# More raw weight tiles and input slots, loads of x and weights ahead of the S5 parameters, roots on GpSimd, in a one-core hybrid block

## The chip, the cores and the metric

One core of a Trainium2 chip runs the whole block in one launch. The metric is the device time in microseconds of that launch. Before the change the median of 3 runs is 1591.73 us (1591.47 to 1593.48). The engines are TensorE (PE; its weight loads are listed apart as PEld), VectorE (DVE), ScalarE (ACT), GpSimd (POOL) and SyncE (SP), which here only issues DMAs.

## The reference

Sequence 1024, width 1024, depth 1, one batch. Cut to what is computed:

```
u = rms_norm(x, norm_mix);  proj = u @ w_in
u_ssm, q, k, v, f_logit, gate_logits = split(proj)        # 512, 512, 512, 512, 8, 2048
y_ssm = gelu(s5_ssm(u_ssm, lam, dt, b, c, d))             # 32 groups of 16, 64 complex states each
glu_a, glu_b = split(y_ssm @ w_glu);  out_a = glu_a * sigmoid(glu_b)
out_b = forgetting_attention(q, k, v, f_logit + b_forget) @ w_fox_o     # 8 heads of 64, causal
gate_a, gate_b = split(sigmoid(gate_logits))
h = x + (gate_a * out_a + gate_b * out_b) @ w_mix_out
h = h + cross_attention(rms_norm(h), rms_norm(mem), w_mem_q, w_mem_kv, w_mem_o)   # 256 tokens, 4 heads
f_a, f_b = split(rms_norm(h) @ w_ffn_in);  h = h + (silu(f_a) * f_b) @ w_ffn_out  # hidden 2816
return rms_norm(h)
```

All is float32.

## The kernel before

**Products.** Every float32 operand of a large product is split in two parts in the matmul type: `hi`, a cast on ACT (L178), and `lo`, the rest, a subtraction on DVE or, where asked for, on GpSimd (L179). A product is then three matmuls, hi·hi, hi·lo and lo·hi (`mm3`, L168 to L170). A weight block goes by DMA into a tile `raw` of the weight pool (0.5 MB for 1024 columns) and from there by a split into `whi` and `wlo`. All places that fetch weights share the tag `raw` with 2 buffers (L150, L383, L559, L803, L1537), so that a load waits until the split two loads before it is done.

**Stages.** `stage_in` normalises and transposes mem and x, computes keys and values of the memory and the S5 input projection. `stage_ssm` computes 32 units of the gates beside the S5 recurrence. Then come the eight heads of forgetting attention, with the Glu products as filler for TensorE, and `stage_tail`: mixing, cross-attention, FFN, output.

**The opening, `stage_in`.** Its work is written as a table of steps, `ORDER_IN` (L41), which is run through from left to right. A letter is the kind of step, what follows is its tile or block (m, n are the two mem tiles, 0 to 7 the x tiles; weights are counted in hexadecimal, so Da and Db are 10 and 11):

- G gain, F fetch of a tile (L349), Q its square sum on ACT (L360), R the root of the mean (L362, for x one for a pair of tiles), S scaling (L217), T transposes on TensorE (L223; half 0 into the one `misc` bank of PSUM, half 1 into `pv`), E their evacuation as hi and lo (`uh`, `ul`)
- D fetch of a weight block (L384): 0 to 3 key columns, 4 to 7 value rows of w_mem_kv, 8 to 11 column blocks of w_in for the S5 input; W its split
- K, k and V, v: key and value products of the memory and their evacuation, ending in stores to `kv_d` (L408, L423)
- U and u: the S5 input product of block q for the half h of the sequence (24 matmuls), and its evacuation; "U10" is block 1, half 0
- L0: 13 small DMAs with the S5 parameters lam, log dt, C, B, d (L1132 to L1148). L1: the transposes of lam and C, through the `misc` bank (L1153, L1160), and their copies on DVE (L1155, L1161). P: the rest of the S5 preparation, mostly on DVE

The framework's scheduler takes this order as priority, and moves single instructions where an engine's operands come later; each engine then runs its own list in order. Tiles of x, mem and the two gains share the tag `xt` with 8 buffers (L347).

**Queues.** SyncE issues nearly all loads, in order. Its DMAs go round eight completion lanes: a DMA waits for the landing of the one that used its lane before. An issue that waits for a free buffer or a lane holds up all that follow it.

**Roots.** `rsqrt` (L187) has two ways. With `pool=True` GpSimd raises to the power -0.5 (L197, with the constant tile `mhalf`) and DVE adds one Newton step of three operations; with `pool=False` DVE makes a first guess on the bits (L199) and three Newton steps (L201 to L203). The four roots for the pairs of x tiles in the opening take the second way, all others the first.

Of the kernel before, what the change touches and what calls it, by code (L numbers as in the profile page):

```python
# [9 lines left out]
F32 = mybir.dt.float32  # L10
# [9 lines left out]
P = 128  # L20
D = 1024
# [10 lines left out]
RAW = 1072  # L32
# [6 lines left out]
RSLOT_LATE = (0, 1, 2, 3, 4, 4, 5, 5, 6, 6, 7, 7)  # L39

ORDER_IN = """  # L41
G0 Fm Qm Fn D1 X24 Qn Rm D0 Sm F1 G1 Tm0 Rn Em0 Sn Tn0 F0 Tm1 W0 Q0 Tn1 En0 F2 Q1 W1g En1 Em1 K0 D2 F3 K1 R0
S0 T00 T01 k0 E00 Q2 W2g D3 E01 D4 S1 T10 Q3 W3 k1 D5 K3 K2 W4 E10 W5 D6 R1 k2 T11 k3 S2 F4 Q4 V0 F5 S3g T30
E11 D7 Q5 F7 T20 R2 T21 E21 E20 S4 E30 W6 W7 T40 V1 D8 S5 E40 W8 T31 V2 L0 T41 E31 V3 D9 Db T50 F6 Q6 v T51 W9
E51 U00 Da Q7 L1 E41 u00 R3 S6 Wa T60 E50 S7 T61 T70 Wbg E61 U10 E60 P0 U20 u10 T71 E70 E71 u20 P1 U21 U11 U30
P2 u30 U31 u11 u31 U01 u21 P3 P4 P5 u01
"""

# [57 lines left out]
class Shared:  # L106
# [5 lines left out]
    def tmp(self, name, dt=F32):  # L112
        return self.pool.tile([P, D], dt, tag="tmp", bufs=4, name=name)
# [5 lines left out]
class Block:  # L119
    BANKS = {"mm": 3, "sc": 2, "pv": 2, "misc": 1}  # L120

    def __init__(self, ctx, tc):
        self.tc, self.nc = tc, tc.nc
        nc = self.nc
        self.V, self.A, self.G, self.T, self.S = nc.vector, nc.scalar, nc.gpsimd, nc.tensor, nc.sync
        self.const = ctx.enter_context(tc.tile_pool(name="const", bufs=1))
        self.small = ctx.enter_context(tc.tile_pool(name="small", bufs=3))
        self.wpool = ctx.enter_context(tc.tile_pool(name="wpool", bufs=4))
        self.dram = ctx.enter_context(tc.tile_pool(name="dram", bufs=1, space=DRAM))
        self.psum = ctx.enter_context(tc.tile_pool(name="psum", bufs=2, space=PSUM))  # L130
        self.ident = self.const.tile([P, P], F32, name="ident")
        make_identity(nc, self.ident)
        self.mhalf = self.const.tile([P, 1], F32, name="mhalf")
        nc.vector.memset(self.mhalf, -0.5)
        self.junk = self.const.tile([P, 512], BF16, name="junk")
        self.nbank = 0
# [197 lines left out]
def stage_in(B, xp, s5, x, mem, g_mix, g_kv, w_in, w_mem_kv, uT, u_d, kv_d):  # L334
# [9 lines left out]
    names = {"m": -2, "n": -1, **{str(t): t for t in range(NT)}}  # L344

    def xtile(name="xt"):
        return xp.tile([P, D], F32, tag="xt", bufs=8, name=name)  # L347

    def fetch(t):  # L349
        tiles[t] = xtile()  # L350
# [9 lines left out]
        A.activation(junk, tiles[t], AF.Square, scale=1.0 / 32, accum_out=ss[t // 2][:, t % 2:t % 2 + 1])  # L360
# [15 lines left out]
    def wget(i):  # L376
        if i < 4:
            src = w_mem_kv[:, i * P:(i + 1) * P]
        elif i < 8:
            src = w_mem_kv[2 * (i - 4) * P:2 * (i - 3) * P, 512:1024]  # L380
        else:
            src = w_in[:, C_U + (i - 8) * P:C_U + (i - 7) * P]
        raw[i] = B.wpool.tile([P, RAW], F32, tag="raw", bufs=2, name="raw")[:, :D]  # L383
        S.dma_start(raw[i].rearrange("p (k c) -> p k c", k=D // src.shape[-1]),  # L384
                    src.rearrange("(k p) c -> p k c", p=P))

# [111 lines left out]
def stage_tail(B, big, s2, sh, x, glu, aT, gate_d, kv_d, w_fox_o, w_mix_out, g_mq, w_mem_q, w_mem_o, g_ffn,  # L498
# [10 lines left out]
    tmp = sh.tmp  # L509
# [46 lines left out]
    def wslots(src, pool_lo):  # L556

        nk = src.shape[0] // P
        raw = B.wpool.tile([P, RAW], F32, tag="raw", bufs=2, name="raw")[:, :D]  # L559
# [240 lines left out]
    raws, wts, ev = {}, {}, {}  # L800

    def w_fetch(j):
        raws[j] = B.wpool.tile([P, RAW], F32, tag="raw", bufs=2, name="raw")[:, :D], tmp("rawb")  # L803
# [615 lines left out]
class Fox:  # L1419
# [109 lines left out]
    def project(self, h):  # L1529
# [4 lines left out]

        def load(behind=None):
            src = lambda c: self.w_in[:, c + h * DH:c + (h + 1) * DH].rearrange("(k p) c -> p k c", p=P)
            raw = self.raw[h] = B.wpool.tile([P, RAW], F32, tag="raw", bufs=2, name="raw")[:, :D]  # L1537
# [273 lines left out]
```

## Time and profile before

| | |
|---|---|
| median of 3 runs | 1591.73 us (1591.47 to 1593.48) |
| span of the profiled execution | 1586.7 us, 5.0 us under the median |
| TensorE busy | 1534.0 us, 97% |
| DVE, ACT, GpSimd busy | 1019.5, 655.2, 254.3 us |
| DMA | 240.86 MB, 152 GB/s over the span |

Busy time says for how long an engine had an instruction running. In a timeline row the first number is the start, the second the time in use, and brackets give the idle time ahead of it and what ended it. `SPq` rows are issues of DMAs by SyncE: their second number is the time until the next could follow, waits included. The chain of waits is the work that ended last, followed back from the end. The granted clock is TensorE's, 1.00 at full speed.

### The profile page before, as it was taken

What the parts mean: (1) busy time and instruction counts of PE and PEld (TensorE: products, weight loads), DVE (VectorE), ACT (ScalarE), POOL (GpSimd) and SP (SyncE); (2) the same over time, 40 slices, a digit from 0 to 9 for tenths busy, and PEclk for the clock granted to TensorE, in tenths of its full rate; (3) what the DMA queues carried; (4) which work ended last, traced back from release to release, by engine and by line L of the source; (5) the groups of instructions that cost most, each with busy time, mean ns of one, the idle gap of its engine ahead of it and who ended that gap; (6) DMA issues with size and microseconds to landing.
All of it is one profiled execution on the core that took longest, in us unless ns stands there. A gap on an engine that the chain in (4) does not pass through costs nothing.

```text
span 1586.7 us, 20446 instructions
## 1 busy us (share of the span) xinstructions
PE 1534.0 (97%) x7313; PEld 1261.3 (79%) x7313; DVE 1019.5 (64%) x1850; ACT 655.2 (41%) x1173; POOL 254.3 (16%) x335
## 2 busy tenths in 40 slices
PE   7799999999999899999999999999999999999997
PEld 6578888898777668888888778888888888788885
DVE  6666445344688687675555697766677776565555
ACT  6422434323576553222435564333333333254342
POOL 2027653200212124110002200100000000000001
PEclk8899999999999999999999999999999999999999
DMA  7764445652023736357412186555444554796642
GB/s 266 125 132 80 127 131 110 130 145 30 18 52 48 186 95 208 125 172 259 160 46 75 54 283 239 170 164 163 155 153 160 166 162 156 261 391 223 195 150 106
DMA packets 197940, 240.86 MB, mean 152 GB/s; under 512 B 35448, under 2 KB 126488, under 8 KB 197328
## 3 DMA queue, kind: packets, MB, share of 16 engines
q1 hardware_dynamic: 191216, 223.84, 48.2%
q10 hardware_dynamic: 6624, 15.73, 2.6%
q8 instruction: 57, 0.93, 0.2%
q14 instruction: 43, 0.35, 0.1%
HBM read 165.60 MB, written 75.86 MB: 152 GB/s over the span
## 4 chain that ended last, share of the span: by engine, by line
PE 75%; DVE 8%; DMA 7%; issue 4%; POOL 3%; ACT 2%; SPq 1%; DVEq 0%; POOLq 0%; ACTq 0%
PE mm L868 14%; PE mm L168 7%; PE pv L868 7%; PE mm L170 7%; PE mm L169 7%; PE mm L1005 4%; PE sc L868 3%; PE sc L1005 3%; PE pv L1005 3%; PE sc L168 3%; PE sc L169 3%; PE sc L170 3%; DMA raw<-in_w_in_dram 2%; PE misc L1005 1%; PE pv L168 1%
## 5 line engine op out<-in xcount | busy, mean ns | idle before, releaser
L179 DVE TENSOR_TENSOR wlo<-raw,whi 128x1024 fp32r<-128x1024 f32 (+2 forms) x121 | 132.0, 1094 | 135.1 <-ACT whi L178 133.9
L178 ACT CAST whi<-raw 128x1024 fp32r<-128x1024 f32 (+2 forms) x124 | 116.1, 940 | 220.0 <-DMA raw<-in_w_ffn_in_dram 54.1
L168 PE MATMUL mm<-uh,whi 128*128 128x512 f32 x344 | 138.8, 404 | 2.8 <-ACT whi L178 2.7
L170 PE MATMUL mm<-uh,wlo 128*128 128x512 f32 x344 | 136.5, 397 | 1.7 <-DVE wlo L179 1.7
L169 PE MATMUL mm<-ul,whi 128*128 128x512 f32 x344 | 136.4, 396 | 0.0
L179 DVE TENSOR_TENSOR ol<-or,oh 128x1024 fp32r<-128x1024 f32 x73 | 89.3, 1224 | 71.6 <-ACT oh L178 70.3
L178 ACT CAST oh<-or 128x1024 fp32r<-128x1024 f32 x73 | 76.8, 1052 | 105.3 <-PE mm L1005 33.6
L900 POOL TENSOR_TENSOR g<-a,c 128x512 f32<-128x512 f32 x22 | 35.2, 1600 | 392.8 <-ACT a L899 373.9
L170 PEld LDWEIGHTS mm<-uh,wlo 128*128 128x128 f32 x344 | 65.7, 191 | 16.5 <-DVE wlo L179 3.1
L1630 POOL TENSOR_TENSOR pl<-pf,ph 128x512 fp32r<-128x512 f32 (+1 forms) x32 | 39.7, 1239 | 241.1 <-DVE ph L1629 196.1
L168 PEld LDWEIGHTS mm<-uh,whi 128*128 128x128 f32 x344 | 65.9, 192 | 15.5 <-ACT whi L178 3.2
L169 PEld LDWEIGHTS mm<-ul,whi 128*128 128x128 f32 x344 | 66.0, 192 | 11.3
L197 POOL TENSOR_TENSOR r<-ms,mhalf 128x1 f32<-128x1 f32 x26 | 15.1, 582 | 354.9 <-DVE ms L193 344.5
L1627 ACT ACTIVATE pf<-sc 128x512 f32<-128x512 f32 (+1 forms) x96 | 46.5, 490 | 46.3 <-DVE sc L1623 28.6
L868 PE MATMUL pv<-S3h,we 128*128 128x512 f32 x176 | 58.1, 389 | 0.0
L1633 DVE TENSOR_TENSOR pl<-pf,ph 128x512 fp32r<-128x512 f32 (+2 forms) x64 | 35.1, 550 | 10.2 <-ACT ph L1632 9.5
L1005 PE MATMUL mm<-oh 128*128 128x512 f32 x106 | 41.2, 389 | 0.0
L1005 PE MATMUL mm<-ol,oh 128*128 128x512 f32 x106 | 41.2, 389 | 0.0
L1005 PE MATMUL mm<-oh,ol 128*128 128x512 f32 x106 | 41.2, 389 | 0.0
L168 PE MATMUL mm<-yh,whi 128*128 128x512 f32 x104 | 40.9, 393 | 0.0
L168 PE MATMUL sc<-uh,whi 128*128 128x512 f32 x104 | 40.8, 393 | 0.0
L170 PE MATMUL mm<-yh,wlo 128*128 128x512 f32 x104 | 40.6, 390 | 0.0
(580 smaller groups left out, 4537.5 us busy)
## 6 DMA issues: line engine op xcount, KB each, us to landing
or<-c_d SPq DMA_DIRECT2D x77, 256.0 KB
raw<-in_w_in_dram SPq DMA_DIRECT2D x22, 512.0 KB
wo<-in_w_ffn_out_dram SPq DMA_DIRECT2D x22, 512.0 KB
c_d<-g SPq DMA_DIRECT2D x44, 256.0 KB
t_d<-wo SPq DMA_DIRECT2D x44, 256.0 KB
or<-t_d SPq DMA_DIRECT2D x44, 256.0 KB
raw<-in_w_ffn_in_dram SPq DMA_DIRECT2D x20, 512.0 KB
rawb<-in_w_ffn_in_dram SPq DMA_DIRECT2D x20, 512.0 KB
```

The costliest lines, as they stand in the source:

```text
L168: T.matmul(ps, lh, rh, start=first, stop=False)
L169: T.matmul(ps, lh, rl, start=False, stop=False)
L170: T.matmul(ps, ll, rh, start=False, stop=last)
L178: self.A.copy(hi, src)
L179: (self.G if pool_lo else self.V).tensor_sub(lo, src, f32(hi))
L197: self.G.tensor_tensor(out=r, in0=v, in1=self.mhalf[:, 0:n], op=ALU.pow)
L868: T.matmul(ps, l_[:, k, :], r_, start=first and k == 0 and i == 0, stop=k == 3 and i == 2, skip_group_check=True)
L900: G.tensor_mul(g[:, 512:], a1, c1)
L1005: T.matmul(ps, l_[:, gi], r_[:, 512:], start=n < 3 and p == 0 and k == 0 or n == 7 and p == 0 and k == 0, stop=p == NP - 1 and k == 2, ski ...
L1627: self.exp = A.activation(pf[:, off:], ps[:, off:], AF.Exp)
L1630: G.tensor_sub(pl[:, off:], pf[:, off:], f32(ph[:, off:]))
L1633: V.tensor_sub(pl[:, off:], pf[:, off:], f32(ph[:, off:]))
```

## The change

- The program is built with a reserve of 1024 bytes for GpSimd's DMAs (L1797), in place of the default.
- The tag `raw` has 4 buffers in all its places, `xt` 11 instead of 8.
- `mhalf` is two wide and `root` no longer asks for the DVE way, so that the four roots of x use GpSimd too.
- `ORDER_IN` is another table: fetches of x tiles and of weight blocks come earlier, L0 later, and a few steps behind them in another place.

```diff
 ORDER_IN = """
-G0 Fm Qm Fn D1 X24 Qn Rm D0 Sm F1 G1 Tm0 Rn Em0 Sn Tn0 F0 Tm1 W0 Q0 Tn1 En0 F2 Q1 W1g En1 Em1 K0 D2 F3 K1 R0
-S0 T00 T01 k0 E00 Q2 W2g D3 E01 D4 S1 T10 Q3 W3 k1 D5 K3 K2 W4 E10 W5 D6 R1 k2 T11 k3 S2 F4 Q4 V0 F5 S3g T30
-E11 D7 Q5 F7 T20 R2 T21 E21 E20 S4 E30 W6 W7 T40 V1 D8 S5 E40 W8 T31 V2 L0 T41 E31 V3 D9 Db T50 F6 Q6 v T51 W9
-E51 U00 Da Q7 L1 E41 u00 R3 S6 Wa T60 E50 S7 T61 T70 Wbg E61 U10 E60 P0 U20 u10 T71 E70 E71 u20 P1 U21 U11 U30
+G0 Fm Qm Fn D1 X24 Qn Rm D0 Sm F1 G1 Tm0 Rn Em0 Sn Tn0 F0 D2 Tm1 W0 Q0 Tn1 En0 F2 F3 D3 Q1 W1g En1 Em1 K0 F4 F5 K1 R0
+S0 T00 T01 k0 E00 Q2 W2g D4 F6 F7 E01 S1 T10 Q3 W3 k1 D5 K3 K2 W4 E10 W5 D6 R1 k2 T11 k3 S2 Q4 V0 S3g T30
+E11 D7 Q5 T20 R2 T21 E21 E20 S4 E30 W6 D8 W7 T40 V1 D9 S5 E40 T31 V2 E31 W8 T41 L0 V3 Da T50 Q6 v T51 W9
+E51 U00 Db Q7 E41 R3 S6 u00 L1 Wa T60 E50 S7 T61 T70 Wbg E61 U10 E60 T71 E70 E71 P0 U20 u10 u20 P1 U21 U11 U30
 P2 u30 U31 u11 u31 U01 u21 P3 P4 P5 u01
 """
@@ Block.__init__
-        self.mhalf = self.const.tile([P, 1], F32, name="mhalf")
+        self.mhalf = self.const.tile([P, 2], F32, name="mhalf")
@@ wload; the same in wget, wslots, w_fetch and project's load
-        raw = self.wpool.tile([P, RAW], F32, tag="raw", bufs=2, name="raw")
+        raw = self.wpool.tile([P, RAW], F32, tag="raw", bufs=4, name="raw")
@@ stage_in
-        return xp.tile([P, D], F32, tag="xt", bufs=8, name=name)
+        return xp.tile([P, D], F32, tag="xt", bufs=11, name=name)
...
-        rs[i] = B.rsqrt(ss[-1][:, i % 2:i % 2 + 1] if i < 0 else ss[i], pool=i < 0)
+        rs[i] = B.rsqrt(ss[-1][:, i % 2:i % 2 + 1] if i < 0 else ss[i])
@@ launch
-    nc = _bacc.Bacc("TRN2", target_bir_lowering=False, num_devices=1)
+    nc = _bacc.Bacc("TRN2", target_bir_lowering=False, num_devices=1, dynamic_dma_scratch_size=1024)
```

SyncE's list in the opening, from the w_in block D8 (after: from the second store of K) to D10. Before, the three `raw` rows on in_w_in are D8 (`raw_523`), D9 (`raw_593`) and D11 (`raw_595`), and the last row is D10:

```order
L384 DMA raw_523<-in_w_in_dram 128x8x128
L1141 DMA craw_556<-in_c_re_dram 128x1x64 x3
L1141 DMA craw_561<-in_c_im_dram 128x1x64 x4
L1146 DMA b_re_566<-in_b_re_dram 128x16x16
L1146 DMA b_im_567<-in_b_im_dram 128x16x16
L1148 DMA dbc_570<-in_d_skip_dram 128x512
L384 DMA raw_593<-in_w_in_dram 128x8x128
L384 DMA raw_595<-in_w_in_dram 128x8x128
L351 DMA xt_602<-in_x_dram 128x1024
L423 DMA kv_d_83<-kv_298 128x1024
L423 DMA kv_d_83<-kv_299 128x1024
L384 DMA raw_650<-in_w_in_dram 128x8x128
```

After, D8 and D9 are `raw_486` and `raw_509`, D10 is `raw_579`; D11 (not shown) follows two more stores to kv_d:

```order
L408 DMA kv_d_83<-kv_297 128x1024
L384 DMA raw_486<-in_w_in_dram 128x8x128
L384 DMA raw_509<-in_w_in_dram 128x8x128
L1132 DMA prow_546<-in_lam_re_dram 16x128
L1133 DMA prow_546<-in_lam_im_dram 16x128
L1135 DMA ldr_549<-in_log_dt_dram 16x2
L1141 DMA craw_551<-in_c_re_dram 128x1x64 x4
L1141 DMA craw_556<-in_c_im_dram 128x1x64 x4
L1146 DMA b_re_561<-in_b_re_dram 128x16x16
L1146 DMA b_im_562<-in_b_im_dram 128x16x16
L1148 DMA dbc_565<-in_d_skip_dram 128x512
L384 DMA raw_579<-in_w_in_dram 128x8x128
```

D8 and D9 now stand together ahead of all parameters, and D10 directly behind them; the x tiles have left this part of the list.

DVE's list around the copies of C's transposes (`cT_re`, `cT_im`). Before, the split of W9 (`wlo_618`) comes ahead of them, that of W10 later:

```order
L179 TENSOR_TENSOR wlo_618<-raw_593,whi_617 128x1024
L179 TENSOR_TENSOR ul1_1_98<-misc_597,uh1_1_90 128x2x128
L1155 COPY par_656<-misc_654 128x48
L248 TENSOR_SCALAR edt_xc_750<-par_656 128x16
L1216 TENSOR_TENSOR den_1052<-par_656 128x16
L249 TENSOR_SCALAR edt_k_751<-edt_xc_750 128x16
L250 TENSOR_SCALAR edt_k_751<-edt_k_751 128x16
L1161 COPY cT_re_658<-misc_660 128x256
```

After:

```order
L1252 TENSOR_TENSOR dbc_565<-dbc_565,msk_1064 128x512
L1155 COPY par_653<-misc_651 128x48
L179 TENSOR_TENSOR wlo_666<-raw_579,whi_665 128x1024
L1161 COPY cT_re_655<-misc_657 128x256
L179 TENSOR_TENSOR ul2_1_100<-pv_679,uh2_1_92 128x2x128
L248 TENSOR_SCALAR edt_xc_739<-par_653 128x16
```

The split of W10 (`wlo_666`) now stands between the copy of lam (`par`) and the copies of C.

ACT's list in attention, at the weights of head 7 (`whi_5057` before, `whi_5033` after) and the first Glu weights (`whi_5628`, `whi_5604`). Before:

```order
L178 CAST whi_5057<-raw_4963 128x1024
L1627 ACTIVATE pf_5070<-sc_5064 128x256
L178 CAST whi_5628<-raw_5625 128x1024
L1632 CAST ph_5068<-pf_5070 128x256
L1562 ACTIVATE hb_3246<-mm_4959 64x512
L1627 ACTIVATE pf_5089<-sc_5083 128x128
L1563 CAST hb_3244<-mm_4959 64x512
L1632 CAST ph_5087<-pf_5089 128x128
L1567 ACTIVATE hb_3247<-mm_4959 64x512
```

After:

```order
L178 CAST whi_5033<-raw_4939 128x1024
L1627 ACTIVATE pf_5046<-sc_5040 128x256
L178 CAST whi_5604<-raw_5601 128x1024
L1632 CAST ph_5044<-pf_5046 128x256
L178 CAST whi_5688<-raw_5685 128x1024
L1627 ACTIVATE pf_5065<-sc_5059 128x128
L1562 ACTIVATE hb_3222<-mm_4935 64x512
L1632 CAST ph_5063<-pf_5065 128x128
L1563 CAST hb_3220<-mm_4935 64x512
L178 CAST whi_5773<-raw_5770 128x1024
L1654 COPY num_4858<-pv_4960 65x512
L1567 ACTIVATE hb_3223<-mm_4935 64x512
```

The second and third Glu weights (`whi_5688`, `whi_5773`) stand here now; before, they came some 40 rows later. Their loads on SyncE stand ahead of head 7's forget rows (L1575) for the same reason.

More of the change, by code (lines that the diff above doesn't have):

```diff
@@ L382, in wget @@
             src = w_in[:, C_U + (i - 8) * P:C_U + (i - 7) * P]
-        raw[i] = B.wpool.tile([P, RAW], F32, tag="raw", bufs=2, name="raw")[:, :D]
+        raw[i] = B.wpool.tile([P, RAW], F32, tag="raw", bufs=4, name="raw")[:, :D]
         S.dma_start(raw[i].rearrange("p (k c) -> p k c", k=D // src.shape[-1]),
@@ L558, in wslots @@
         nk = src.shape[0] // P
-        raw = B.wpool.tile([P, RAW], F32, tag="raw", bufs=2, name="raw")[:, :D]
+        raw = B.wpool.tile([P, RAW], F32, tag="raw", bufs=4, name="raw")[:, :D]
         S.dma_start(raw.rearrange("p (k c) -> p k c", k=nk), src.rearrange("(k p) c -> p k c", p=P))
@@ L802, in w_fetch @@
     def w_fetch(j):
-        raws[j] = B.wpool.tile([P, RAW], F32, tag="raw", bufs=2, name="raw")[:, :D], tmp("rawb")
+        raws[j] = B.wpool.tile([P, RAW], F32, tag="raw", bufs=4, name="raw")[:, :D], tmp("rawb")
         for r_, c in zip(raws[j], (0, FH)):
@@ L1536, in load @@
             src = lambda c: self.w_in[:, c + h * DH:c + (h + 1) * DH].rearrange("(k p) c -> p k c", p=P)
-            raw = self.raw[h] = B.wpool.tile([P, RAW], F32, tag="raw", bufs=2, name="raw")[:, :D]
+            raw = self.raw[h] = B.wpool.tile([P, RAW], F32, tag="raw", bufs=4, name="raw")[:, :D]
             rv = raw.rearrange("p (k c) -> p k c", k=8)
```

## The prediction

> **What bounds the kernel now.** I read the page first, then busy time by stretches, the idle times of TensorE in the opening, and what SyncE's queue does there. The page:
>
> ```profile
> span 1586.7 us, 20446 instructions
> PE 1534.0 (97%) x7313; PEld 1261.3 (79%) x7313; DVE 1019.5 (64%) x1850; ACT 655.2 (41%) x1173; POOL 254.3 (16%) x335
> ...
> L168 PE MATMUL mm<-uh,whi 128*128 128x512 f32 x344 | 138.8, 404 | 2.8 <-ACT whi L178 2.7
> ```
>
> TensorE is busy 1534.0 of 1586.7 us, and the change takes away none of its work. So the most that anything here can give is 52.7 us of idle time, and the time lost to a low clock. Where that lies shows in busy time by stretches (columns: us, each engine's busy time and instructions, granted clock, DMA share, GB/s):
>
> ```profile
> 0.00:20.00 20.00, 12.11 (x53) 9.14 (x54) 9.19 (x30) 10.85 (x17) 5.84 (x13) 0.74 0.81 275
> 20.00:40.00 20.00, 18.85 (x129) 17.43 (x128) 18.68 (x42) 14.26 (x28) 4.80 (x2) 0.92 0.76 256
> 40.00:60.00 20.00, 14.87 (x69) 11.99 (x69) 12.57 (x25) 7.81 (x16) 0.00 (x0) 0.91 0.88 126
> 60.00:80.00 20.00, 15.60 (x60) 11.60 (x59) 13.69 (x46) 10.47 (x14) 3.21 (x1) 0.83 0.54 121
> 80.00:100.00 20.00, 18.32 (x85) 15.27 (x86) 19.86 (x102) 5.05 (x9) 0.77 (x1) 1.00 0.63 131
> 480.00:540.00 60.00, 56.51 (x268) 42.17 (x266) 45.66 (x114) 37.62 (x71) 11.79 (x10) 0.97 0.47 99
> 540.00:600.00 60.00, 54.54 (x256) 39.48 (x255) 46.09 (x95) 33.34 (x64) 12.29 (x9) 1.00 0.54 142
> 600.00:1500.00 900.00, 891.78 (x4051) 735.05 (x4050) 600.22 (x905) 350.48 (x646) 89.01 (x70) 1.00 0.54 179
> ```
>
> The opening (0 to 100 us) has 20.3 us of TensorE idle and a clock under 1 (from 40 to 80 us, 0.91 and 0.83 cost 20 x 0.09 + 20 x 0.17 = 5.2 us); attention (480 to 600) has 9.0 us; the 900 us behind it have 8.2 in all. The opening's idle times, on TensorE's timeline (brackets: idle before, and what ended it):
>
> ```profile
> 53.83 1.01 PE L223 MATMUL misc<-ident,xt 128*128 128x128 f32 x4 [4.62 <-DVE ul L179]
> 65.10 0.31 PE L1153 MATMUL misc<-ident,prow 48*128 48x48 f32 x1 [3.08 <-issue]
> 66.64 0.78 PE L170 MATMUL mm<-uh,wlo 128*128 128x512 f32 x1
> 76.86 0.50 PE L170 MATMUL mm<-uh,wlo 128*128 128x512 f32 x1 [1.21 <-DVE wlo L179]
> 81.68 0.63 PE L223 MATMUL misc<-ident,xt 128*128 128x128 f32 x4 [1.80 <-DVE ul L179]
> ```
>
> 10.7 us lie between 49 and 82 us, where the S5 input projection (steps U) waits for weights. After the long gaps matmuls run slow too: 0.78 us in the row at 66.64, against a mean of 0.40 for this shape (the page's group of L168). The chain of waits says what they wait for, and SyncE's queue why:
>
> ```profile
> 38.84 9.74 DMA raw<-in_w_in_dram
> 51.76 8.97 DMA raw<-in_w_in_dram
> 64.70 8.15 DMA raw<-in_w_in_dram
> 72.88 2.01 ACT whi L178
> 74.91 1.90 DVE wlo L179
> ```
>
> ```profile
> 34.54 3.10 SPq L408 DMA_DIRECT2D kv_d<-kv  x2
> 37.70 0.43 SPq L384 DMA_DIRECT2D raw<-in_w_mem_kv_dram  x1
> 38.84 0.38 SPq L384 DMA_DIRECT2D raw<-in_w_in_dram  x1
> 39.27 4.72 SPq L1141 DMA_DIRECT2D craw<-in_c_re_dram  x3
> 44.04 3.58 SPq L1141 DMA_DIRECT2D craw<-in_c_im_dram  x4
> 51.76 1.12 SPq L384 DMA_DIRECT2D raw<-in_w_in_dram  x2
> 52.98 4.93 SPq L351 DMA_DIRECT2D xt<-in_x_dram  x1
> ```
>
> The chain is three w_in loads in a row: D8 issued at 38.84 and landed at 48.6, D9 issued at 51.76 and landed at 60.7, D10 issued at 64.70 and landed at 72.85. D9 is not late for want of data: 12.5 us pass between the issues, in which SyncE issues S5 parameters one by one. D10 waits until the split of D9 (at 64.7) gives back one of two raw tiles.
>
> **The change, part by part.**
>
> *Four raw tiles.* D10's issue no longer waits for the split of D9. In the order of the changed kernel it stands behind the parameters, and waits on older splits only. Cost nothing; the gain is in the next step.
>
> *Loads in another order.* D5, D6, D7 and all x tiles come before the parameters; D8 and D9 too. D8 now stands right behind the kv_d stores of K (issued from 34.54 on before, and as before they wait for K): I take its issue at 35.4, and 8.2 to 9.7 us to landing as in the chain: 43.6 to 45.1, against 48.6. D9 takes D5's tile, free by 38.84 at the latest, since D8's issue there waited for the later split of D6; it queues behind D8 and lands 3 to 5 us after it, 47 to 50, against 60.7. But now SyncE stands at the fifth C load until D9 has landed (the completion lane it needs is D9's), and the rest of the parameters goes from there. Before, from the first c_im issue (44.04) to the weight load behind the parameters (51.76) took 7.7 us; with nothing to wait for, seven issues at 0.4 to 0.5 us (the row at 38.84) take 3. So D10 is issued at 50 to 58, and lands 8.2 to 9.0 us later and not before the b loads queued ahead of it: 60 to 67, against 72.85; I take 64.5, nearer to the upper end, since in 40 to 60 us, full of the same small pieces, only 126 GB/s moved. This is the term that decides.
>
> *What then ends the wait.* The split of D10 takes 2.0 us on ACT and 1.9 on DVE (72.88 to 76.8 in the chain): done at 64 to 71, I take 68.4. In the new order DVE's copy of C's transpose stands behind that split, and TensorE's U10 stops after 6 of 24 matmuls until the copy (about 0.5 us) has freed the one misc bank. So TensorE, now ahead with U00 and part of U10, idles there and goes on at a low clock. From this release to the second half of the third unit (U21) are 18 matmuls of U10, 24 of U20 and three turns of x6 and x7. The chain has both at full clock, at the start of U21:
>
> ```profile
> 84.60 0.44 PE pv L223 x4
> 85.03 0.23 PE mm L168
> ```
>
> 42 matmuls by 0.23 are 9.7 us, three turns by 0.44 are 1.3, and 1 to 2 us more go to the low clock (half of what two such stops cost before, 5.2). 68.4 + 0.5 + 11.0 + 1.6 puts U21's start at 81.5 to 82, with 76 and 85 as ends; before it was 85.03. Gain 3 us, bounds 0 and 9. What stands next in line: D11 lands last (behind two kv_d stores), and its split is ahead of the evacuation of x6's turn on ACT; that is why I don't take the lower end.
>
> *x tiles early.* Before, the square of the last tiles waited for x:
>
> ```profile
> 66.80 1.06 ACT L360 ACTIVATE junk<-xt 128x1024 bf16<-128x1024 f32 x1 [3.76 <-DMA xt<-in_x_dram]
> 7.89 0.55 POOL L197 TENSOR_TENSOR r<-ms,mhalf 128x1 f32<-128x1 f32 x1 [6.09 <-DVE ms L195]
> 32.51 2.41 POOL L215 TENSOR_TENSOR xt<-xt,gain 128x1024 f32<-128x1024 f32 x1 [8.74 <-ACT xt L214]
> 33.48 1.46 DVE L201 TENSOR_TENSOR rt<-r 128x2 f32<-128x2 f32 x1
> 19.96 0.16 DVE L203 SCALAR_TENSOR_TENSOR r<-rt,r 128x2 f32<-128x2 f32 x1
> ```
>
> All of them now are there by about 30 us, so the last squares and roots leave the stretch behind 66.80. What this is worth to the gap of 1.80 at 81.68 is in the term above. More x bytes before 30 us share DMA with D2 to D7: the first 20 us moved at 275 GB/s and 40 to 60 at 126, so there is room, and I cost it 0, bounds -1.9 and +1.9 (0.5 MB at 275 GB/s).
>
> *Roots on GpSimd.* Each of four roots loses seven or eight DVE operations of 0.16 us (row at 19.96), 1.2 us, and gains one GpSimd operation of 0.55 (row at 7.89). DVE is busy 18.68 of 20 us from 20 to 40, so part of the 4.8 us of all four may reach TensorE: -0.7, bounds -1.6 and +2.2 (four times 0.55, each in TensorE's way). The row at 33.48 speaks against it: a DVE operation on two elements took 1.46 us, and ended when the GpSimd multiply of 32.51 did (34.92). The Trainium skill, "SBUF — State Buffer", section "SBUF: two separate sides", states that a DVE operation with two SBUF inputs and a GpSimd operation that reads SBUF exclude each other for a whole instruction. The row agrees; by that rule four GpSimd roots would block DVE four times for up to 0.55 us, 2.2 us, about half of what they save, and the sum would be the same within 1 us.
>
> *Memory given back by the smaller reserve.* The kernel issues no DMA from GpSimd (the page's queues are hardware ones), so 0.
>
> *Raw tiles behind the opening.* In the gate stage a load now waits on the split four before; TensorE is full there: 0. In attention two more Glu weights are loaded where the row at 519.02 stands, ahead of it, and split right behind the first (523.18), where they were split from 555.28 on:
>
> ```profile
> 519.02 0.44 SPq L1575 DMA_DIRECT2D hb<-cum_d  x1
> 522.64 0.50 PE L168 MATMUL mm<-uh,whi 128*128 128x512 f32 x1 [2.74 <-ACT whi L178]
> 523.18 1.05 ACT L178 CAST whi<-raw 128x1024 fp32r<-128x1024 f32 x1 [0.18 <-DMA raw<-wg_d]
> ...
> 527.78 0.59 ACT L1567 ACTIVATE hb<-mm 64x512 fp32r<-64x512 f32 x1 [1.79 <-DVE hb L1566]
> ...
> 555.28 1.05 ACT L178 CAST whi<-raw 128x1024 fp32r<-128x1024 f32 x1
> ```
>
> That is 2.1 us of ACT moved ahead of attention's evictions, and as much taken out of 540 to 600, which has 5.5 us of idle. I take -0.5, bounds -3 and +4. In the 900 us from 600 on: 0, bounds -1 and +1.5.
>
> *Sum:* -3 - 0.7 - 0.5 = -4.2 us on the profiled execution's 1586.7 us of span. The median of 1591.73 lies 5.0 us above that span (what lies around it), which I keep: 1591.7 - 4.2 = 1587.5.
>
> One rule that would give another sum: the Trainium skill, "DMA: Bandwidth & Descriptors", section "Specifications", puts line rate at pieces of 512 B and above. The w_in columns come in such pieces, yet moved in stretches of 121 to 131 GB/s, against 275 at the start; no run here shows which part of that is the parameters' small pieces. If the rule holds for w_in alone, it is the next rival.
>
> **The rivals.** *The parameters were all that slowed w_in.* Issued ahead of them, D8 and D9 move at 275 GB/s, 1.9 us each behind 3.8 us of kv_d stores (1 MB): landed by 41 and 43, and D10, with 3 us of issue and 7 us at most behind the b loads, by 53. TensorE then loses neither the 10.7 us nor the 5.2 of clock, 15.9 at most; some 10 with one stop left for C's copy: 1576 to 1582. Against it: the load issued at 64.70, behind no parameters, still took 8.15 us.
>
> *The wait only moves.* D9 at 50 and the parameters behind it as slow as before (39.27 to 51.76, 12.5 us) issue D10 at 62.5, landed at 71.5, and U21 starts at 75.4 + 0.5 + 11.0 + 1.6 = 88.5, 3.5 us late; from a landing at 67.5 (U21 at 84.5) on nothing is gained. With -1.2 of the other terms: 1590 to 1594, no change. For it speaks the place of the copy behind the split of D10; against it, that most of the 12.5 us were waits on loads issued just before.
>
> *Slower: attention.* Two more loads of 0.5 MB are issued ahead of head 7's forget rows and row maximum, and the third split stands on ACT ahead of that head's evictions (527.78). At 99 GB/s, as 480 to 540 ran, 1.05 MB take 10.6 us from 519, so they land at 529.6, 2 us late at the eviction; from about 5 us late (533) on scores and products both stand, and the row maxima, sums and broadcasts of the last heads follow each other, so that the lateness comes twice or more: +7 to +14 with the opening's gain of 4 against it, 1595 to 1602. Against it: half of the DMA time of this stretch is free (share 0.47).
>
> **How the numbers follow.** No change is what a measurement of this kernel can't tell from it, 0.2%, 3.2 us: 1588.5 to 1594.9. Forecast (1583 to 1590): 0.50, of which 0.07 lie above 1588.5. Unblocked: 0.13. Moved: 0.17. Slower: 0.20. Faster 0.43 + 0.13 = 0.56, same 0.07 + 0.17 = 0.24, slower 0.20. The range leaves out half of the unblocked and half of the slow case: 1579 to 1597. The forecast's own range is 1583 to 1590.
>
> **What would show it.** Right: D8 landed by 45, D9 by 50, D10 at 60 to 67; no square waits for x after 35 us; the 4.62 us gap is gone, and one of 3 to 7 us stands inside U10, ended by the copy of C's transpose; U21 starts at 80 to 84; TensorE's idle time from 480 to 600 stays within 3 us of 9.0. Wrong: D10 beyond 68, a stop on ACT before 533 at a Glu weight, or a gap behind 600 that was not there.

## The result, and the profile after

The changed kernel takes 1590.62 us (median of 14 runs, 1587.63 to 1597.87), the kernel before 1592.08 (14 runs beside them): a ratio of 0.9992, 95% interval 0.9982 to 1.0002. That is no change that can be told from none. The opening did get shorter, by what was forecast or more; nearly all of it was given back behind it. The profiled execution took 1593.75 us with a span of 1592.0, so that 1.7 us lie around the span. It lies 3.1 us above its kernel's median, and that of before (a span of 1586.7, and some 2.0 us around it as in before's second profile below) about 3.3 us below: the two totals say nothing against each other, and the profiles are compared stage by stage.

The page of after, its first two lines on the whole:

```profile
span 1592.0 us, 20434 instructions
...
PE 1538.3 (97%) x7313; PEld 1265.5 (79%) x7313; DVE 1023.0 (64%) x1822; ACT 655.8 (41%) x1173; POOL 257.4 (16%) x339
```

Busy time by stretches of after, the stretches of the prediction and two new ones, 218 to 242 us, in which the third block of the S5's input is due (columns as before: us; PE, PEld, DVE, ACT, POOL busy; granted clock, DMA share, GB/s):

```profile
0.00:20.00 20.00, 12.20 (x53) 9.28 (x54) 8.88 (x22) 12.03 (x19) 8.28 (x15) 0.73 0.97 316
20.00:40.00 20.00, 18.79 (x129) 17.44 (x128) 17.44 (x31) 15.49 (x31) 5.97 (x4) 0.92 0.77 269
40.00:60.00 20.00, 14.51 (x65) 11.71 (x64) 13.30 (x28) 9.20 (x18) 0.69 (x1) 0.83 0.70 111
60.00:80.00 20.00, 17.36 (x86) 13.71 (x85) 16.40 (x69) 7.62 (x13) 2.88 (x1) 1.00 0.82 188
80.00:100.00 20.00, 20.00 (x90) 16.57 (x89) 16.29 (x72) 4.21 (x6) 4.63 (x7) 1.00 0.41 103
218.00:230.00 12.00, 12.00 (x67) 10.33 (x66) 2.67 (x5) 1.58 (x3) 4.92 (x7) 1.00 0.99 95
230.00:242.00 12.00, 7.11 (x28) 6.08 (x27) 4.67 (x7) 3.52 (x9) 5.13 (x5) 0.72 0.73 215
480.00:540.00 60.00, 55.65 (x257) 41.13 (x256) 46.51 (x112) 37.50 (x72) 9.86 (x9) 0.94 0.45 97
540.00:600.00 60.00, 56.39 (x266) 40.89 (x267) 46.97 (x104) 33.45 (x65) 13.19 (x12) 1.00 0.57 151
600.00:1500.00 900.00, 890.85 (x4045) 734.53 (x4044) 605.01 (x908) 351.64 (x648) 90.72 (x70) 1.00 0.54 178
```

From 40 to 100 us TensorE idles 8.1 us instead of 11.2, and the clock costs 3.4 us (all in 40 to 60) instead of 5.2. Together 4.9 us: the opening's gain. In 230 to 242 us stands a hole that was not there before: 4.9 us idle, and a mean clock of 0.72.

The idle times of TensorE in after's opening, from its timeline:

```profile
51.27 1.09 PE L223 MATMUL misc<-ident,xt 128*128 128x128 f32 x4 [5.49 <-DVE ul L179]
66.50 0.44 PE L1160 MATMUL misc<-ident,craw 128*128 128x128 f32 x2 [0.81 <-DVE cT_re L1161]
72.42 0.63 PE L223 MATMUL misc<-ident,xt 128*128 128x128 f32 x4 [1.83 <-DVE ul L179]
```

The 3.08 us at 65 have shrunk to 0.81, those at 76.86 are gone, those at 81.68 come 9 us earlier; the 4.62 at 53.83 have become 5.49 at 51.27. SyncE's queue (first fence) and ACT's splits of D8 to D11 (second fence) of after:

```profile
36.08 2.65 SPq L384 DMA_DIRECT2D raw<-in_w_in_dram  x2
...
48.43 2.52 SPq L1141 DMA_DIRECT2D craw<-in_c_im_dram  x4
...
55.24 0.37 SPq L384 DMA_DIRECT2D raw<-in_w_in_dram  x1
57.27 1.57 SPq L423 DMA_DIRECT2D kv_d<-kv  x2
58.90 0.83 SPq L384 DMA_DIRECT2D raw<-in_w_in_dram  x1
```

```profile
46.94 1.91 ACT L178 CAST whi<-raw 128x1024 fp32r<-128x1024 f32 x1 [4.28 <-DMA raw<-in_w_in_dram]
49.28 1.97 ACT L178 CAST whi<-raw 128x1024 fp32r<-128x1024 f32 x1
62.16 1.97 ACT L178 CAST whi<-raw 128x1024 fp32r<-128x1024 f32 x1 [2.39 <-DMA raw<-in_w_in_dram]
69.61 1.94 ACT L178 CAST whi<-raw 128x1024 fp32r<-128x1024 f32 x1 [0.90 <-DMA raw<-in_w_in_dram]
```

D8 is there at 46.9, D9 by 49.3, D10 at 62.1, D11 at 69.6. The end of the opening is read from one instruction that every kernel has, the first gate product. Before (first fence) and after (second):

```profile
112.12 0.39 PE L168 MATMUL sc<-uh,whi 128*128 128x512 f32 x1
```

```profile
106.92 0.39 PE L168 MATMUL sc<-uh,whi 128*128 128x512 f32 x1
```

5.2 us are gained there. At the third product of the S5's input with `F` (line 1361), before and after:

```profile
236.22 1.95 PE L1361 MATMUL pv<-xg,F 128*128 128x128 f32 x16
```

```profile
235.43 3.75 PE L1361 MATMUL pv<-xg,F 128*128 128x128 f32 x16 [4.89 <-DMA xg<-u_d]
```

At this product 0.8 us of the gain is left. Most of the rest went in one wait, for the DMA that brings `xg` (L1354), and the 16 products behind it take 3.75 us instead of 1.95, at the low clock that follows the wait.

The same reading (the start of one and the same instruction, kernel against kernel, stage by stage) gives this table; each number is how much longer the stage took than in the first profile of before, in us:

| stage | after | after, run again | before, run again |
|---|---|---|---|
| opening, to the first gate product | -5.2 | -3.9 | +0.2 |
| S5 and gates, to the last gate product | +7.4 | +5.3 | -0.1 |
| attention, from there to its last product | +1.4 | -0.6 | +1.9 |
| mixing: the fox_o products | +1.6 | +1.3 | 0.0 |

### The profile page after: what moved, and what is told of

Read it like the earlier page. It is cut to its first block, busy times and chain, and to the rows that moved or that the text cites. A ratio compares the mean times of both kernels' runs of the same rounds, so it can differ in the third digit from the quotient of the medians.

```text
span 1592.0 us, 20434 instructions
## 1 busy us (share of the span) xinstructions
PE 1538.3 (97%) x7313; PEld 1265.5 (79%) x7313; DVE 1023.0 (64%) x1822; ACT 655.8 (41%) x1173; POOL 257.4 (16%) x339
## 4 chain that ended last, share of the span: by engine, by line
PE 79%; DVE 7%; DMA 6%; ACT 3%; POOL 2%; issue 2%; SPq 1%; DVEq 0%; POOLq 0%; ACTq 0%
PE mm L868 15%; PE mm L168 8%; PE mm L169 8%; PE mm L170 8%; PE pv L868 7%; PE mm L1005 4%; PE sc L868 4%; PE sc L168 3%; PE sc L170 3%; PE sc L169 3%; PE sc L1005 3%; PE pv L1005 3%; PE misc L1005 1%; DMA raw<-in_w_in_dram 1%; DMA raw<-in_w_mem_kv_dram 1%
## 5 line engine op out<-in xcount | busy, mean ns | idle before, releaser
L179 DVE TENSOR_TENSOR ol<-or,oh 128x1024 fp32r<-128x1024 f32 x73 | 89.3, 1224 | 70.8 <-ACT oh L178 69.6
L197 POOL TENSOR_TENSOR r<-ms,mhalf 128x1 f32<-128x1 f32 (+1 forms) x30 | 17.9, 597 | 373.0 <-DVE ms L193 345.6
L1100 POOL TENSOR_TENSOR sg<-sg,ga 128x512 f32<-128x512 f32 x16 | 29.9, 1890 | 73.3 <-DVE sg L1093 73.0
```

Of the source, the lines that this page charges most:

```text
L179: (self.G if pool_lo else self.V).tensor_sub(lo, src, f32(hi))
L1100: self.B.G.tensor_mul(self.out[j][:, cs], self.out[j][:, cs], ga)
```

## The experiments

Each kernel was timed beside runs of the kernel before on the same chip; ratios are to those, with 95% intervals. Line numbers of these kernels differ from the profile's by up to 4 where lines were added.

**The two kernels again.** No edit.

> The kernel before, unchanged, to learn how far executions of one program differ and where. Both theories: ratio 1.000, within 0.2%. If the spread of 1587 to 1597 us comes from loads that land now earlier, now later in the S5 stage, this profile should show at xg (the S5 input of one block, L1354) or in attention another idle time than the first one did (1.55 us and 0 there), by 1 us or more.

> The changed kernel, unchanged. Theory A (the opening's 5 us are kept, and what the first profile lost behind it, 7.4 us in the S5 stage with 4.89 of them ahead of the xg product, is one slow load): here the opening is again 5 us ahead at the first gate product, and the S5 stage loses under 2 us; ratio 0.997 to 0.999. Theory B (the S5 stage always takes the 5 us back, since TensorE now reaches the xg product before its load): again 4 us or more of idle time at the third xg product; ratio 1.000.

Before: 1592.17 us against 1590.70, 1.0012 (1.0001 to 1.0022). The same program thus differs from itself by 0.12% in one comparison, and its profile had a span of 1592.7 us, where the first had 1586.7. The 6 us between the two executions lie in attention (+1.9) and behind it; the opening and the S5 stage repeat within 0.2 us (the wait for the second `xg` is 1.44 us, 1.55 in the first profile). After: 1590.77, 1.0000 (0.9990 to 1.0009), and the hole is there again:

```profile
235.88 3.63 PE L1361 MATMUL pv<-xg,F 128*128 128x128 f32 x16 [4.04 <-DMA xg<-u_d]
```

So the opening's gain and the S5 stage's loss belong to the change, though their size differs by 1.3 and 2.1 us between after's two profiles, and what attention does cannot be told from single profiles.

**The opening alone, and the rest alone.** In the first kernel everything of the change is kept, but only the opening has four raw tiles (two of them from the input pool); behind it the tag `raw` has two as before. In the second the opening is that of before, with two tiles of its own, and everything behind it has four.

```diff
 e_open, against the changed kernel: wload, wget, wslots, project's load
-        raw = self.wpool.tile([P, RAW], F32, tag="raw", bufs=4, name="raw")
+        raw = self.wpool.tile([P, RAW], F32, tag="raw", bufs=2, name="raw")
 w_fetch
-        raw[i] = B.wpool.tile([P, RAW], F32, tag="raw", bufs=4, name="raw")[:, :D]
+        raw[i] = (B.wpool.tile([P, RAW], F32, tag="raw", bufs=2, name="raw")[:, :D] if i % 2 else
+                  xp.tile([P, D], F32, tag="rawx", bufs=2, name="raw"))
 e_rest, against the kernel before: bufs=4 and the reserve of 1024 as in the change, and in w_fetch
+        raw[i] = xp.tile([P, D], F32, tag="rawx", bufs=2, name="raw")
```

> The changed opening alone: new order, eleven slots, roots on GpSimd and four raw tiles there (two of them from the opening's own pool), but two raw tiles again behind it. Theory A (opening -5, four tiles behind it cost 2 to 4): 0.9965, that is 1586 to 1588 us, faster than the whole change. Theory B (S5 takes the gain back whatever the number of tiles): 0.999 to 1.000, as the whole change. Theory C (the four tiles behind the opening cost nothing): ratio equal to that of the whole change within 0.1%.

> The opening of before with its order and its own two raw tiles, and four raw tiles behind it (and the small reserve, without which they don't fit). Theory A: slower by 2 to 4 us, 1.0015 to 1.0025. Theory C: 1.000, within 0.1%. The forecast had -0.5 us for it, with bounds -4 and +5.5.

The opening alone: 1586.90 us, 0.9976 (0.9965 to 0.9987), faster, as theory A had it. The first gate product starts at 107.49, 4.6 us earlier than before, and the third `xg` product does not wait:

```profile
231.78 1.95 PE L1362 MATMUL pv<-xg,F 128*128 128x128 f32 x16
```

The rest alone: 1599.35 us, 1.0053 (1.0035 to 1.0070), slower, by more than twice what theory A had. It loses 4.8 us in the S5 stage, of which this wait is the larger part (here the second block: its load stands behind gate weights that SyncE issued at 183.26):

```profile
195.03 3.57 PE L1361 MATMUL pv<-xg,F 128*128 128x128 f32 x16 [3.67 <-DMA xg<-u_d]
```

and 2.0 at the fox_o products, where TensorE waits for DVE's evictions:

```profile
716.04 0.50 PE L168 MATMUL pv<-ath,whi 128*128 128x512 f32 x1 [1.62 <-DVE gb L531]
```

Its opening is 1.8 us longer than before, too. So four tiles behind the opening lose time. Why just the third `xg` is late in after was open: that its load was slow by chance fell with the second run of after, which shows the same. What the traces show ahead of it is which gate weights are loaded. The gates take w_in in eight pairs of column blocks, numbered 0 to 7 (each pair has 256 columns and comes by two loads of 0.5 MB in pieces of 1 KB). With two tiles, pair 6 is issued just ahead of the third `xg`; with four, the loads run one pair further ahead, and it is pair 7. In the stretch 218 to 230 us, of the opening alone (first fence) and of after (second), the DMA traffic by queue:

```profile
q1 hardware_dynamic: 1390, 2.31, 77.7%
```

```profile
q1 hardware_dynamic: 877, 0.88, 92.4%
```

Columns: packets, MB, share of 16 engines. With pair 6, 1390 packets in 77.7% of the engines' time, 0.11 us each; with pair 7, 877 in 92.4%, 0.20 us each (0.924 x 16 x 12 / 877), although its packets are the smaller ones in the mean (1.0 KB against 1.7). The issues that the profile lists there are of the same kinds and sizes, but for one more store of 0.25 MB in the quicker stretch. Two experiments take this up below.

**Parts of the opening.** The opening alone (0.9976) with one of its parts undone, and the whole change with two tiles everywhere:

```diff
 o_noroot, against e_open
-        rs[i] = B.rsqrt(ss[-1][:, i % 2:i % 2 + 1] if i < 0 else ss[i])
+        rs[i] = B.rsqrt(ss[-1][:, i % 2:i % 2 + 1] if i < 0 else ss[i], pool=i < 0)
 o_oldorder, against e_open: ORDER_IN of the kernel before
 o_two, against the changed kernel, in all its places
-  tag="raw", bufs=4
+  tag="raw", bufs=2
```

> The changed opening alone (two raw tiles behind it), but the four roots of x on DVE as before. The forecast had 0.7 us for the roots: 0.998 to 0.9985 against 0.9976 with them. If GpSimd's roots block DVE as much as they save it: 0.9976. If they free DVE fully: 1.000.

> The old order of the opening with four raw tiles there, eleven slots and the roots on GpSimd; two raw tiles behind it. Theory T (tiles): D10 is issued at 61 instead of 64.7 us, since it no longer waits for the split of D9, ratio 0.998 to 0.9985. Theory O (order): 1.000, since the parameters still hold D9 back to 51.8 us.

> The new order, eleven slots and the roots on GpSimd, with two raw tiles everywhere. Theory T (the order needs the tiles): D8 to D10 wait for splits again and the parameters behind them are later than before, ratio 1.000 to 1.003. Theory O (the order alone does it): 0.9976, and the first gate product again 4 to 5 us ahead of before.

| kernel | median us | ratio | first gate product | against before |
|---|---|---|---|---|
| opening alone | 1586.90 | 0.9976 (0.9965 to 0.9987) | 107.49 | -4.6 |
| its roots on DVE | 1589.64 | 0.9994 (0.9986 to 1.0003) | 112.68 | +0.6 |
| its order that of before | 1589.02 | 0.9989 (0.9979 to 0.9999) | 109.25 | -2.9 |
| the change with two tiles | 1591.27 | 1.0002 (0.9990 to 1.0013) | 110.95 | -1.2 |

Without the roots nothing is left of the gain, with the old order a part. With two tiles the median shows none, and a first gate product 1.2 us earlier in one profile is no more than after's own two profiles differ by. In the old order the four tiles let D10 be issued at 58.52 us, where before had 64.70: theory T, though the gain is smaller than it said. The roots' way is seen in DVE's list. The root of the last pair of x tiles is followed by their scaling; with the roots on GpSimd (opening alone):

```profile
44.75 0.16 DVE L202 SCALAR_TENSOR_TENSOR rt<-rt,ms 128x2 f32<-128x2 f32 x1
54.85 0.15 DVE L203 SCALAR_TENSOR_TENSOR r<-rt,r 128x2 f32<-128x2 f32 x1
...
55.29 1.28 DVE L217 SCALAR_TENSOR_TENSOR xt<-xt,r,gain 128x1024 f32<-128x1024 f32 x1
```

and on DVE:

```profile
36.59 0.24 DVE L203 SCALAR_TENSOR_TENSOR r<-rt,r 128x2 f32<-128x2 f32 x2
57.08 0.16 DVE L201 TENSOR_TENSOR rt<-r 128x2 f32<-128x2 f32 x1
...
61.02 0.16 DVE L203 SCALAR_TENSOR_TENSOR r<-rt,r 128x2 f32<-128x2 f32 x1
61.22 1.28 DVE L217 SCALAR_TENSOR_TENSOR xt<-xt,r,gain 128x1024 f32<-128x1024 f32 x1
```

The steps are 0.16 us each, but they do not stand side by side: between two of them DVE's list has evacuations and splits that wait for weights. With more steps to go when the splits begin, this scaling comes 5.9 us later, and TensorE waits 2.90 us at the turn of C and 3.88 at one of the last x tiles, where the opening alone waits 1.99 at the latter and nowhere else over 0.5 us from there to the end of the opening. That the number of steps is the cause is read from these lists; no run changed it by itself. The two waits with the roots on DVE:

```profile
67.50 0.44 PE L1161 MATMUL misc<-ident,craw 128*128 128x128 f32 x2 [2.90 <-DVE cT_re L1162]
77.62 0.63 PE L223 MATMUL misc<-ident,xt 128*128 128x128 f32 x4 [3.88 <-DVE edt_p L255]
```

**The roots alone, on the kernel before.**

```diff
-        self.mhalf = self.const.tile([P, 1], F32, name="mhalf")
+        self.mhalf = self.const.tile([P, 2], F32, name="mhalf")
-        rs[i] = B.rsqrt(ss[-1][:, i % 2:i % 2 + 1] if i < 0 else ss[i], pool=i < 0)
+        rs[i] = B.rsqrt(ss[-1][:, i % 2:i % 2 + 1] if i < 0 else ss[i])
```

> The kernel before with one thing changed: the four roots of the x tiles in the opening are taken on GpSimd. Theory A (the roots were on DVE's path to the first products of x, whatever the order of the loads): the first gate product starts 3 to 5 us earlier than in the kernel before (at 107 to 109 us instead of 112.1), ratio 0.997 to 0.998. Theory B (the roots only matter in the new order, where the x tiles come early; in the old one the weights set the opening's end): the first gate product stays within 1 us of 112.1, ratio 0.9995 to 1.0005. Rival by my forecast's sum: 0.7 us.

1590.86 us, 1.0001 (0.9989 to 1.0012), and the first gate product at 111.86, 0.3 us earlier than before. That is theory B's number: in the old order with two tiles the roots are worth nothing. Its reason, the order, is not shown: the old order with four tiles and the roots on GpSimd, in the table above, gained 2.9 us. So neither the roots alone (-0.3) nor the new order, tiles and slots without them (+0.6) do anything, and together they give 4.6 us.

**Two gate pairs in exchanged order.** The changed kernel, pairs 6 and 7 exchanged, so that with four tiles pair 6 stands ahead of the third `xg` again, and pair 7 some 28 us earlier. Everything that is computed stays the same.

```diff
+    place = (0, 1, 2, 3, 4, 5, 7, 6)
-        w[p] = [B.wblock(w_in, 4 * n, 4, C_G + 256 * p, 256) for n in range(2)]
+        w[p] = [B.wblock(w_in, 4 * n, 4, C_G + 256 * place[p], 256) for n in range(2)]
-        A.dma_start(gate_d[j * P:(j + 1) * P, 512 * h:512 * h + 512], gs)
+        jj = 2 * place[j // 2] + j % 2
+        A.dma_start(gate_d[jj * P:(jj + 1) * P, 512 * h:512 * h + 512], gs)
```

> The changed kernel with the last two of the eight column pairs of the gates swapped: with four raw tiles the load issued ahead of the third xg is then that of pair 6, which in the kernel with two tiles stood at this place and moved 207 to 249 GB/s, in place of pair 7, which moved 84 to 94. Theory P (pair 7's load is slow wherever it stands; with four tiles it came ahead of xg): the idle time of 4.0 to 4.9 us at the third xg product goes, pair 7 is slow at its earlier place, ratio 0.997 to 0.998. Theory Q (any load there delays xg once there are four tiles): idle time 4 us again, ratio 1.000.

1583.31 us, 0.9959 (0.9946 to 0.9973): faster than both kernels, and by more than theory P had. The third `xg` product does not wait:

```profile
229.41 1.95 PE L1364 MATMUL pv<-xg,F 128*128 128x128 f32 x16
```

The stretch with pair 7's load (first row, 189 to 201 us) and that with pair 6's and `xg` (second):

```profile
189.00:201.00 12.00, 12.00 (x55) 9.94 (x54) 10.77 (x14) 1.71 (x3) 4.05 (x5) 1.00 0.95 119
217.00:229.00 12.00, 12.00 (x67) 10.31 (x66) 2.96 (x5) 1.58 (x3) 4.92 (x7) 1.00 0.96 227
```

Pair 7 is slow at its new place as well, 119 GB/s at a DMA share of 0.95, and holds up nothing there; TensorE is full in both stretches. In after the stretch 189 to 201 us, with pair 6 in it, moved 143 GB/s at a share of 0.57.

**The mirror: the same exchange with two tiles.** The same edit on the kernel with the opening alone, where it puts pair 7 ahead of the third `xg`.

> The kernel that has only the opening of the change (four raw tiles there, two behind it) with the last two column pairs of the gates, 6 and 7, in exchanged order. With two tiles the sixth pair's load stands directly ahead of the third block of the S5's input, and with the exchange that is now pair 7. Theory P (pair 7 is a slow load wherever it stands, about 85 to 95 GB/s, and the block behind it comes late): the third block is issued at its usual time and lands 15 us later instead of 11, the third xg product waits 3 to 5 us where the unexchanged kernel waited 0, and the ratio to before rises from 0.9976 to 1.000 (0.998 to 1.002). Rival Q (the exchange is good in itself, for instance because pair 6's data is wanted earlier): no wait, ratio 0.9976 or under.

1591.62 us, 0.9999 (0.9986 to 1.0011), against 0.9976 without the exchange. The stretches, the product on TensorE's timeline, and its `xg` in the chain of waits:

```profile
218.00:230.00 12.00, 12.00 (x67) 10.32 (x66) 2.83 (x5) 1.80 (x4) 4.39 (x6) 1.00 0.92 95
230.00:242.00 12.00, 7.77 (x37) 6.70 (x36) 4.89 (x7) 4.07 (x10) 5.93 (x6) 0.86 0.70 204
```

```profile
235.39 3.53 PE L1365 MATMUL pv<-xg,F 128*128 128x128 f32 x16 [4.23 <-DMA xg<-u_d]
```

```profile
219.82 15.43 DMA xg<-u_d
```

The wait is made with two tiles, by the order of two column pairs alone, with 95 GB/s as in after. So after's wait comes with pair 7 directly ahead of the third `xg`, and the four tiles make it because they bring pair 7 there: of the four kernels with two or four tiles and either order, the two with pair 7 at this place wait.

The rest alone shows the limits of this. There, too, pair 7 stands directly ahead of the third `xg` and is slow (227 to 240 us: 110 GB/s at a DMA share of 1.00), but TensorE, late by then, comes to the product 15.5 us after the issue of `xg` at 227.31 and does not wait:

```profile
242.84 1.95 PE L1361 MATMUL pv<-xg,F 128*128 128x128 f32 x16
```

Its own wait, at the second block, has another cause: `xg`, behind pair 5, lands within 10.0 us as elsewhere, but its issue at 184.87 is late. The gate weights ahead of it wait for two splits on DVE, which start at 182.02 us, in before at 176.35, although the stage began only 1.8 us later. What four tiles change there in DVE's list was not tested.

**The splits of w_mix_out.** The other loss behind the opening: with four tiles the second half of w_mix_out is loaded, and so split, earlier. DVE's list in after, at the fox_o products (`wlo` and `wbl` are splits, `gb` and `sg` the evictions, L531 and L532):

```profile
709.16 1.23 DVE L179 TENSOR_TENSOR wbl<-raw,wbh 128x1024 fp32r<-128x1024 f32 x1 [1.55 <-ACT wbh L178]
710.90 0.68 DVE L531 TENSOR_TENSOR gb<-gb,pv 128x512 f32<-128x512 f32 x1
711.50 1.22 DVE L179 TENSOR_TENSOR wlo<-raw,whi 128x1024 fp32r<-128x1024 f32 x1
712.63 0.68 DVE L532 TENSOR_TENSOR sg<-sg,gb 128x512 f32<-128x512 f32 x1
713.24 0.68 DVE L531 TENSOR_TENSOR gb<-gb,pv 128x512 f32<-128x512 f32 x1
```

A split in wait for ACT (1.55 us idle, then 1.23) holds up the eviction behind it, and TensorE waits for that one:

```profile
711.63 0.50 PE L168 MATMUL pv<-ath,whi 128*128 128x512 f32 x1 [0.57 <-DVE gb L531]
```

The edit, on the kernel with the exchanged pairs, holds these splits until the sum of that part is formed:

```diff
-            V.tensor_add(sg[:, cs], sg[:, cs], gb)
+            fox["sum"] = V.tensor_add(sg[:, cs], sg[:, cs], gb)
-        B.split(*hl, raw, pool_lo)
+        with B.behind(fox["sum"]):
+            B.split(*hl, raw, pool_lo)
```

> The changed kernel with the gate pairs 6 and 7 exchanged (0.9959), and beside it the splits of the second half of w_mix_out are held until the sum of the fox part's products is formed, as they were with two raw tiles. Theory (the splits stand ahead of the evictions on DVE and ACT and stop TensorE): the loss of 1.3 to 2.0 us at the end of the fox_o products is gone, no wait on DVE L531 over 0.3 us there, ratio 0.995 (0.9935 to 0.9965). Rival (the splits have to be made somewhere, and wait where they now stand): the same 1.5 us is lost at the first w_mix_out products, ratio 0.996 to 0.997.

1581.91 us, 0.9945 (0.9928 to 0.9962), the fastest of all. The stage that lost 1.6 us with the exchange alone loses 0.0, TensorE does not wait for the evictions there, and the stage behind it is as long as without the edit (+0.1 in both): the splits find room. The gain in the total, 0.14% or 2.2 us, fits, but the two intervals overlap, so it is the stage that shows it.

## Why the prediction was right, and where it was not

The median, 1590.62 us, lies in the range and 3.1 us above the forecast; the case that came is "no change", which had 0.24, and not by the rival that was to bring it. The sum was -4.2. It was made of a term for the opening that came out about right, by steps of which several were wrong, and of zeros behind it that were not zeros. That the median lies in the range, 1579 to 1597, is luck as far as the mechanism goes: the loss that decided the result stood at nothing in the sum, and the forecast's own range, 1583 to 1590, does not hold it.

- **The base.** The prediction laid the 5.0 us between span and median to what lies around the span. That is 1.7 us in after and 2.0 in before's second profile. The rest is the distance of that execution from its kernel's median; since the forecast was the median less the sum, nothing hung on it.
- **"I take 64.5" for D10, and U21 at 81.5 to 82.** D8 landed at 46.9, 1.8 us later than forecast (10.8 us for a load, not 8.2 to 9.7). D9 was there by 49.3 (47 to 50 forecast), D10 was issued at 55.2 (50 to 58) and landed at 62.1 (60 to 67), 2.4 us before the value taken. No square waits for x after 35 us: the last one starts at 33.65. From U21 to the first gate product TensorE is full, 27.1 us before (85.03 to 112.12); 106.92 less that puts U21 at 79.8, just under the 80 to 84 that was to show the forecast right. The opening gained 5.2 and 3.9 us in the two profiles of after, against 3 + 0.7.
- **"The 4.62 us gap is gone": wrong.** It is 5.49, at 51.27. D8's split stands on ACT and DVE ahead of the evacuation of an x tile's turn, for which the next turn waits, as it did before, and D8 landed only 1.7 us earlier; the wait is as long and begins sooner. That no chain of this kind would be left was read from the landings alone, not from the lists.
- **"One of 3 to 7 us stands inside U10": right place, wrong size.** It is 0.81 us. TensorE had lost its time at 51 us already, and D10 was there 2.4 us before the value taken.
- **D11 behind two kv_d stores, its split ahead of the evacuation of x6's turn: as feared.** The 1.83 us at 72.42 are that, with the split at 69.61 ahead of it.
- **"Roots on GpSimd ... -0.7": this step failed.** The term was sized by the 0.16 us that each step takes on DVE, and added to the others (seven steps fewer for each root, as after's page shows with 28 DVE instructions less; the GpSimd operation took 0.70 us, not 0.55). In the runs it is a condition of them: 5.2 us (112.68 against 107.49) with the new order and four tiles, 0.3 in the kernel before. By DVE's list, what counted was not the time of the steps but how many of them stood behind other work when the last pair came. The rule of the Trainium skill that the prediction weighed against this step ("SBUF — State Buffer", section "SBUF: two separate sides": the two engines exclude each other) does show: in after a DVE step on two elements took 2.24 us beside GpSimd's split of 2.42 (row below). But with the roots on DVE one such step took 2.39 us at the same place: it holds up either way of taking the root, and does not decide.

```profile
18.98 2.24 DVE L202 SCALAR_TENSOR_TENSOR rt<-rt,ms 128x2 f32<-128x2 f32 x1
```

- **"In the gate stage a load now waits on the split four before; TensorE is full there: 0": this step failed, and it decided the result.** It cost 7.4 and 5.3 us. The prediction asked whether TensorE waits there for weights. It did not ask what stands on SyncE's queue behind the weights that now come earlier: `xg`, whose load met a slow pair ahead of it, so that TensorE waited 4.9 and 4.0 us.
- **"In the 900 us from 600 on: 0, bounds -1 and +1.5": wrong by 1.3 to 1.6 us** at the fox_o products, the upper bound. The earlier load brought an earlier split, ahead of evictions on DVE: the gap behind 600 us that was to show the forecast wrong.
- **Attention, -0.5.** TensorE's idle time from 480 to 600 is 8.0 us (9.0 before, within the 3 us allowed). But a stop on ACT before 533 us at a Glu weight, a sign of being wrong, did come: ACT waits 1.27 us for the second one (row below), in after's second run 1.34, and the kernels with two tiles do not have that wait. TensorE then waits 1.06 us at 531.08 for ACT. The stage's length differs from the first profile of before by -0.6 to +4.0 us over the kernels with two tiles (eight profiles, before's own two among them) and by -0.6 to +1.8 over five with four: neither harm nor gain can be told from the spread. So the mechanism of the rival "slower: attention" shows, far smaller than it was sized (+7 to +14); the time that it forecast did not come.

```profile
529.14 1.04 ACT L178 CAST whi<-raw 128x1024 fp32r<-128x1024 f32 x1 [1.27 <-DMA raw<-wg_d]
```

- **"The parameters were all that slowed w_in": did not come.** D8, ahead of all parameters, took 10.8 us.
- **The rule of the Trainium skill on line rate** ("DMA: Bandwidth & Descriptors", section "Specifications": pieces of 512 B and above), read as all that line rate takes, would have both pairs move alike. The traces do not agree with that reading: the stretch with pair 7's pieces of 1 KB moved 95 GB/s with the engines busy for 0.99 of the time, that with pair 6's, of the same size, 225.

What stays open is why pair 7 is slow. Where it is placed and how many tiles there are do not make it so; it differs from pair 6 only in its columns. Nor is it settled where the 0.31% come from by which the last kernel lies below the opening alone, though both have the opening's gain and neither has the two losses: in their profiles it is 1.0 us in the S5 stage, 1.6 in attention and 2.5 behind 930 us, and the last two are no more than the two profiles of before differ by there.

## What to carry to other kernels

More buffers for a tag that loads, splits and evictions share do not only let loads start earlier: they put them, and the splits that follow, ahead of other work in two in-order lists. So ask, for each stage that uses the tag, what stands next on the issuing queue and on the splitting engine, not only who waits for the load. Parts of a change that meet in one list are not added: here the roots alone gave 0.3 us, the new order, tiles and slots without them nothing, and all together 4.6. And a profile's total is one draw (before's spans were 1586.7 and 1592.7), while the start of one instruction, kernel against kernel, repeated within 0.2 us through the opening and the S5 stage in before, and within 1.3 us at the end of the opening in after; so it tells a loss of 5 us, stage by stage, where the total does not.

## What the runs showed of the hardware

Loads of the same size and shape from one matrix, 2 x 0.5 MB in pieces of 1 KB, differ by the columns: in the stretch with pair 7, some 95 GB/s at a DMA share of 0.92 to 0.99 in after and in the mirror; with pair 6 in the same stretch, 225 at 0.86. Read as time for a packet, 0.20 us against 0.11. The slow rate follows the pair to another place (119 GB/s) and to another kernel.

The granted clock falls with one wait: in after, with 4.9 us idle from 230.5 us on, it is 0.50 from 235.4 to 241.4 us and 1.00 again from 243 on, and 16 products that take 1.95 us took 3.75. After waits of 4.0 and 4.2 us (after's second run, the mirror) the stretch 230 to 242 has 0.86. The S5 stage became 7.4 us longer by a wait of 4.9.
